# Writing a table of routing weights in 192 ordered parts instead of 24 large ones

## The chip, the cores and the metric

The kernel runs on one core of one Trainium2 chip. The metric is device time in microseconds (us). Before the change it is 3143.48 us, the median of three runs (3142.44 to 3146.86).

## The reference, cut to what matters

One transformer layer on 512 tokens of width 2048: a modulated norm, a mixer of attention and a linear recurrence, and then a layer of 16384 experts (PEER), of which each of 8 heads of a token chooses 16. The change lies in the expert layer:

```python
e = (jnp.take_along_axis(i1, ic // PEER_TOPK, axis=-1) * PEER_N_KEYS
     + jnp.take_along_axis(i2, ic % PEER_TOPK, axis=-1))
w = jax.nn.softmax(vs, axis=-1).astype(h.dtype)
...
ug = jnp.take(u, ex, axis=0)
act = jax.nn.gelu(jnp.einsum('thkd,td->thk', ug, hx)) * wx
vg = jnp.take(vt, ex, axis=0)
return jnp.einsum('thk,thkd->td', act, vg)
```

So an output row is a sum over the chosen experts of gelu(u . h) times the routing weight times a row of `v`.

## The kernel before, in words

The program is traced with a tile framework: pools hand out buffers, and every engine has its own in-order queue. The order within a queue is not the order of the source. The framework's scheduler (`schedule_with_timeline_sim`) lays it out by a model of time, moves an instruction ahead when its operands are ready in that model, and keeps true dependencies with semaphores. An instruction whose semaphore hasn't come holds up what stands behind it on its queue. Plain DMAs are issued from SyncE's queue (SP), indirect ones from GpSimd's (POOL).

The 512 tokens are four tiles of 128. Tile 0 of the expert layer takes its rows by direct gathers (`side_work`); three tiles go the dense way. For these the 16384 experts are 128 blocks of 128. `ublock(b)` computes gelu(u . h) of one block for 384 tokens: for each half of the 2048 columns, `stream` (line 96) loads 512 KB of `peer_u` into one of four `raw` buffers on SyncE (line 98), ScalarE casts it to `shi` (line 93), VectorE makes the rest `slo` (line 94), and TensorE runs 24 matmuls of 128x384 (line 689), three for each of 8 column groups: `shi` with `dh`, `shi` with `dl`, `slo` with `dh`. After each half `pump()` runs the lists in `todo`, which advance the direct gathers by GRATE = 0.9 (VectorE uses one gathered row with a pass of 128x2048, lines 755 and 757) and a list of scatters. After both halves ScalarE applies the gelu (line 693) and two DMAs on SyncE put the result into the DRAM tables `tab2` and `tab1` (lines 695 and 697). `ublocks(n)` runs blocks until n are done.

Beside each block's gelu values the tables hold the routing weights, half a tile of tokens (TH = 64) at a time. `halves_of` (line 892) builds them in `ws`, 128 x 128 x 64 floats, single-buffered, in 16 steps: one-hot matrices on VectorE (lines 906 and 911), four matmuls (line 912) and a copy (line 913) each, with ublocks between the steps. At the end four DMAs of 1 MB write `ws` to the table (line 917); each consists of 4096 runs of 256 bytes, and a maximum over the tokens is taken of each quarter (line 918). There are six such half tiles: four ahead of block 75, two after block 81. Between these, lines 928 to 938 do the top-k of the last tile, with loads of `s12` and four more blocks.

Nothing in this kernel pins the order on SyncE. When all blocks are done, the tables are gathered and multiplied with rows of `v` (line 988).

Of the kernel before, what the change touches and what calls it, by code (L numbers as in the profile page):

```python
# [58 lines left out]
def program(ctx: ExitStack, tc: tile.TileContext, a):  # L59
    nc = tc.nc  # L60
# [31 lines left out]
    def hilo(hi, lo, src):  # L92
        A.copy(hi, src)  # L93
        V.tensor_tensor(out=lo, in0=src, in1=hi, op=OP.subtract)  # L94

    def stream(src, n=1024):
        r = raw.tile([128, 1024], F32, name="raw")
        nc.sync.dma_start(r[:, :n], src)
        hi = hl.tile([128, 1024], F32R, name="shi")
        lo = hl.tile([128, 1024], F32R, name="slo")  # L100
        hilo(hi[:, :n], lo[:, :n], r[:, :n])
        return hi, lo

    def three(ah, al, bh, bl):
        return ((ah, bh), (ah, bl), (al, bh))

    def rstd(pool, ss, n, scale):
        v = pool.tile([128, 16], F32, name="rs", tag="rs", bufs=4)[:, :n]
        A.activation(v, ss, AF.Sqrt, bias=eps, scale=scale)
        V.reciprocal(v, v)  # L110
        return v
# [23 lines left out]
    for half in range(2):  # L135
        r = raw.tile([128, 1024], F32, name="raw")[:1]
# [28 lines left out]
    def bank():  # L165
        return ps.tile([128, 512], F32, name="ps", tag="ps")

    def pbank():
        return ps.tile([128, 512], F32, name="pj", tag="pj", bufs=2)

    for q in range(4):
        p = pbank()
# [7 lines left out]
    with tc.tile_pool(name="pro", bufs=1, reuse_waits="tile") as pro:  # L180
# [7 lines left out]
        for t in range(NT):  # L188
# [7 lines left out]
            r = rstd(pro, ss, 1, 1.0 / D)  # L196
            dg = pro.tile([128, 128], F32, name="dg", bufs=2)
            V.tensor_scalar(dg, ident, r, None, op0=OP.mult)
            for k4 in range(4):
                p = pbank()  # L200
# [7 lines left out]
        for k in range(KC):  # L208
            ada(1, k)
            ada(0, k)  # L210
            A.activation(xT[:, k], xT[:, k], AF.Identity, bias=mod[:, 0, k:k + 1], scale=gsc[0][:, k:k + 1])
            A.copy(hh[k], xT[:, k])
            V.tensor_tensor(out=hlo[k], in0=xT[:, k], in1=hh[k], op=OP.subtract)
            wh, wl = stream(a["w_pro"][k], PRO * 128)
            for i, (l, r) in enumerate(three(wfh, wfl, hh[k], hlo[k])):
                PE.matmul(pf[:8], l[:, k * 8:k * 8 + 8], r, start=(k == 0 and i == 0), stop=(k == KC - 1 and i == 2))
            for j in range(PRO):
                for i, (l, r) in enumerate(three(wh, wl, hh[k], hlo[k])):
                    PE.matmul(pacc[j], l[:, j * 128:j * 128 + 128], r, start=(k == 0 and i == 0),  # L219
                              stop=(k == KC - 1 and i == 2))  # L220
# [42 lines left out]
    p = pbank()  # L263
# [9 lines left out]
    p = bank()  # L273
# [19 lines left out]
    def proj(blk):  # L293
        p = pbank()
        b = W_AT[blk] - PRO
        for half in range(2):
            wh, wl = stream(a["w_in"][b, half])
            for k8 in range(8):
                k = half * 8 + k8
                for i, (l, r) in enumerate(three(wh, wl, hh[k], hlo[k])):  # L300
                    PE.matmul(p, l[:, k8 * 128:k8 * 128 + 128], r, start=(k == 0 and i == 0),  # L301
                              stop=(k == KC - 1 and i == 2))
        return p
# [215 lines left out]
    for q in range(4):  # L519
# [8 lines left out]
        for k2 in range(KC // 2):  # L528
            w = stream(a["w_out"][q, k2])
            if q == 3 and k2 >= KC // 2 - HELD:  # L530
                held += [(k2 * 2, *w), (k2 * 2 + 1, *w)]
                continue
            for k in (k2 * 2, k2 * 2 + 1):
                for t in range(NT):
                    out_mm(t, k, *w)
            if q < 3:
                some_ada(1)
        for t in range(NT):
# [10 lines left out]
            if q == 3:  # L549
                s4 = const.tile([128, 1], F32, name="s4", bufs=4)  # L550
                V.tensor_reduce(s4, ssq[:, t], axis=AX.X, op=OP.add)
                w = const.tile([128, 128], F32, name="dg", bufs=4)
# [6 lines left out]
    with tc.tile_pool(name="wk2", bufs=12, reuse_waits="tile") as wk2:  # L559
        for q in range(4):  # L560
            pr = bank()
            for k4 in range(4):
                k = q * 4 + k4
                p = bank()
# [80 lines left out]
    for h in range(H):  # L645
# [6 lines left out]
        for half in range(2):  # L652
            p = pbank()
# [10 lines left out]
            p = bank()  # L664
            c0 = half * 128
# [16 lines left out]
    def ublock(b):  # L682
        p = pbank()
        for half in range(2):
            uh, ul = stream(a["peer_u"][b, half])
            for k8 in range(8):
                k = half * 8 + k8
                for i, (l, r) in enumerate(three(uh, ul, dh[k], dl[k])):
                    PE.matmul(p[:, :NDT], l[:, k8 * 128:k8 * 128 + 128], r, start=(k == 0 and i == 0),  # L689
                              stop=(k == KC - 1 and i == 2))  # L690
            pump()
        ge = gq.tile([128, NDT], F32, name="ge")
        A.activation(ge, p[:, :NDT], AF.Gelu_apprx_tanh)  # L693
        rows = slice(128 + b * 128, 256 + b * 128)
        nc.sync.dma_start(tab2[rows].rearrange("p (t x) -> p t x", t=2)[:, :, 0:128],
                          ge[:, 128:384].rearrange("p (t x) -> p t x", t=2))
        nc.sync.dma_start(tab1[rows, 0:128], ge[:, 0:128])
# [6 lines left out]
    todo = []  # L704

    def pump():
        for f in todo:
            f()

    def ublocks(upto):  # L710
        while blk[0] < upto:
            ublock(blk[0])
            blk[0] += 1
# [76 lines left out]
    def scatter_some(n):  # L790
        for _ in range(n):
            if scatters:
                scatters.pop(0)()

    todo.append(lambda: side.send(GRATE))
    todo.append(lambda: scatter_some(1))
    for t in (1, 2):
# [34 lines left out]
    def make_list(lt, Fs, n):  # L832
# [5 lines left out]
        fs = [lt.tile([128, 128], F32, name=f"lu{i}") for i in range(len(Fs))]  # L838
        for f, F in zip(fs, Fs):
            V.scalar_tensor_tensor(out=f, in0=F, scalar=0.0, in1=iota1, op0=OP.is_gt, op1=OP.mult)  # L840
        if len(Fs) == 1:
# [51 lines left out]
    TH = 64  # L893
    sets = {}

    def halves_of(dz, t, o, tab, c0, lo, step):
        Fs = []
        for hf in range(2):
            h0 = hf * TH
            ws = dz.tile([128, NB, TH], F32, name="ws")  # L900
            for t4 in range(TH // 4):
                ublocks(lo + hf * step + t4 * (step - 3) // (TH // 4))
                p = bank()
                o1 = dz.tile([128, 4, 128], F32, name="o1", bufs=2)
                t0 = h0 + t4 * 4
                V.tensor_tensor(out=o1, in0=iota[:, None, :].to_broadcast([128, 4, 128]),
                                in1=o[:, 0, t0:t0 + 4, None].to_broadcast([128, 4, 128]), op=OP.is_equal)
                for j in range(4):
                    tt = t0 + j
                    o2 = dz.tile([128, 128], F32, name="o2", bufs=6)  # L910
                    V.tensor_scalar(o2, iota, o[:, 1, tt:tt + 1], o[:, 2, tt:tt + 1], op0=OP.is_equal, op1=OP.mult)
                    PE.matmul(p[:, j * 128:j * 128 + 128], o2, o1[:, j], start=True, stop=True)  # L912
                A.copy(ws[:, :, t4 * 4:t4 * 4 + 4].rearrange("p i t -> p t i"), p.rearrange("p (t i) -> p t i", t=4))
            F = dz.tile([128, NB], F32, name="F", bufs=4)
            for i in range(4):
                sl = slice(i * 32, i * 32 + 32)
                nc.sync.dma_start(tab[128 + i * 4096:4224 + i * 4096, c0 + h0:c0 + h0 + TH].rearrange("(i p) t -> p i t", p=128), ws[:, sl])
                V.tensor_reduce(F[:, sl], ws[:, sl], axis=AX.X, op=OP.max)
            Fs.append(F)
        V.tensor_tensor(out=Fs[0], in0=Fs[0], in1=Fs[1], op=OP.max)  # L920
        return Fs[0]

    with tc.tile_pool(name="dz", bufs=1, reuse_waits="tile") as dz:
        Fs = [halves_of(dz, t, oT[t], tab2, t * 256 + 128, B0 + 2 * t * BH, BH) for t in range(2)]
        sets[0] = make_list(dz, Fs, 0)
# [11 lines left out]
    with tc.tile_pool(name="dz2", bufs=1, reuse_waits="tile") as dz:  # L937
        sets[1] = make_list(dz, [halves_of(dz, 0, oT[2], tab1, 128, B0 + 4 * BH + 6, BL)], 1)
        ublocks(NB)
# [106 lines left out]
    def inv(t):  # L1046
        ss = fin.tile([128, 1], F32, name="fss", bufs=4)
        V.tensor_reduce(ss, ssf[:, t], axis=AX.X, op=OP.add)
        return rstd(fin, ss, 1, 1.0 / D)
# [63 lines left out]
    r = inv(1)  # L1113
# [75 lines left out]
```

## Time and profile before

| what | value |
| --- | --- |
| median of three runs | 3143.48 us |
| the profiled execution's own time | 3144.75 us |
| span of the profiled execution | 3142.9 us |
| TensorE's mean granted clock in it | 0.958 |
| starts of the 2048 matmuls with `slo` of the blocks, first and last | 1076.0 and 2382.1 us |
| the `peer_u` loads (SyncE) | 256, 512 KB each |
| writes of `ws` (SyncE) | 24, 1024 KB each |

Times in the profile count from the start of the span. PE is TensorE, PEld its weight load, DVE VectorE, ACT ScalarE, POOL GpSimd, SP SyncE; a "q" behind an engine's name is its instruction queue, where issuing a DMA or waiting on a semaphore takes place. In a row of a timeline stand the start, the duration, engine, line, operation, what it writes and reads, the count of instructions that were merged (xN), and in brackets the idle time before it and what ended it. A line such as L93 or L94 is that of a helper, so its rows are told apart by the tiles.

### The profile page before, as it was taken

The numbers are of one execution on the slowest core, as the hardware profiler recorded it, in microseconds if no ns is written. First come the engines' busy times: TensorE is split into PE (matmuls) and PEld (weight loads), VectorE is DVE, ScalarE is ACT, GpSimd is POOL, SyncE is SP. The second block draws the span as 40 slices with busy tenths as digits, with TensorE's granted clock in tenths as the row PEclk, the third lists the DMA queues.
The fourth block names the chain that finished last, engine by engine and source line by source line (L and its number), as shares of the span: only waits on it lengthen the run. The fifth ranks groups of instructions, "written<-read, shape, count | busy, mean of one in ns | idle before, by whom it ended". The sixth has DMA issues, their size and how long they took to land.

```text
span 3142.9 us, 39160 instructions
## 1 busy us (share of the span) xinstructions
PE 2872.5 (91%) x14093; PEld 2501.5 (80%) x14093; DVE 2487.0 (79%) x4100; ACT 1220.9 (39%) x1653; POOL 944.1 (30%) x673
## 2 busy tenths in 40 slices
PE   7899999989999999988878999889998899988887
PEld 5677777778788899988868999879996688766665
DVE  6877777763368899999989998968888866677787
ACT  5322223662232333433322343413223455556665
POOL 0000000000020033222242322264447645567774
PEclk9999899999999999999988999989999999999998
DMA  9867777333322389999989999989999977779896
GB/s 343 291 222 235 239 236 238 106 107 128 114 90 94 117 297 379 340 306 295 294 270 357 351 347 352 314 319 404 404 403 386 386 278 272 260 270 344 320 327 228
DMA packets 329503, 869.31 MB, mean 277 GB/s; under 512 B 125682, under 2 KB 181362, under 8 KB 274388
## 3 DMA queue, kind: packets, MB, share of 16 engines
q0 software_dynamic: 72512, 477.03, 40.4%
q1 hardware_dynamic: 256352, 389.52, 36.8%
q8 instruction: 112, 1.84, 0.2%
q14 instruction: 91, 0.75, 0.1%
q10 hardware_dynamic: 436, 0.18, 0.0%
HBM read 805.38 MB, written 61.25 MB: 276 GB/s over the span
## 4 chain that ended last, share of the span: by engine, by line
PE 53%; DVE 17%; DMA 15%; issue 8%; ACT 3%; POOL 2%; SPq 1%; DVEq 0%; POOLq 0%; ACTq 0%
PE pj L689 25%; DMA araw<-w_ada 8%; PE ps L988 7%; PE pj L659 6%; DVE slo L94 5%; PE ps L525 4%; DVE gr L757 3%; PE pj L301 2%; PE ps L219 2%; DMA raw<-tab,ig 2%; DVE araw L147 2%; PE ps L912 2%; PE pj L988 1%; PE pj L525 1%; DMA tab<-ws 1%
## 5 line engine op out<-in xcount | busy, mean ns | idle before, releaser
L689 PE MATMUL pj<-dh,slo 128*128 128x384 f32 x2048 | 698.3, 343 | 59.4 <-DVE slo L94 57.9
L689 PE MATMUL pj<-dh,shi 128*128 128x384 f32 x2048 | 699.1, 341 | 29.0 <-ACT shi L93 26.4
L689 PE MATMUL pj<-dl,shi 128*128 128x384 f32 x2048 | 694.8, 339 | 1.3 <-issue 1.3
L93 ACT CAST shi<-raw 128x1024 fp32r<-128x1024 f32 (+1 forms) x402 | 418.3, 1048 | 634.1 <-PE pj L689 219.0
L94 DVE TENSOR_TENSOR slo<-raw,shi 128x1024 fp32r<-128x1024 f32 (+1 forms) x402 | 485.1, 1214 | 214.3 <-ACT shi L93 200.1
L689 PEld LDWEIGHTS pj<-dh,slo 128*128 128x128 f32 x2048 | 392.1, 192 | 70.6 <-DVE slo L94 68.7
L94 DVE TENSOR_TENSOR slo<-gr,shi 128x1024 fp32r<-128x1024 f32 x342 | 407.2, 1220 | 39.6 <-ACT shi L93 38.1
L689 PEld LDWEIGHTS pj<-dh,shi 128*128 128x128 f32 x2048 | 393.0, 192 | 30.9 <-ACT shi L93 27.9
L93 ACT CAST shi<-gr 128x1024 fp32r<-128x1024 f32 x342 | 345.0, 1046 | 157.0 <-PE ps L988 99.2
L743 POOL DMA_INDIRECT gr<-u_rows,ei x128 | 196.0, 1531 | 690.5 <-DVE gr L757 319.6
L689 PEld LDWEIGHTS pj<-dl,shi 128*128 128x128 f32 x2048 | 392.3, 192 | 2.1 <-issue 2.0
L988 PE MATMUL ps<-shi,gh 128*128 128x512 f32 x740 | 277.7, 418 | 64.3 <-ACT gh L93 36.7
L147 DVE SCALAR_TENSOR_TENSOR araw<-araw,sil 128x1024 f32<-128x1024 f32 x192 | 233.7, 1222 | 104.8 <-DMA araw<-w_ada 101.5
L755 DVE SCALAR_TENSOR_TENSOR y<-gr,dots,y 128x2048 f32<-128x2048 f32 x128 | 300.3, 2346 | 13.9 <-DMA gr<-v_rows,ei 12.6
L988 PE MATMUL ps<-slo,gh 128*128 128x512 f32 x740 | 298.0, 411 | 14.6 <-DVE slo L94 13.8
L743 POOL DMA_INDIRECT gr<-v_rows,ei x128 | 211.7, 1654 | 311.4 <-DVE y L755 204.6
L757 DVE SCALAR_TENSOR_TENSOR gr<-gr,hrow 128x2048 f32<-128x2048 f32 x128 | 291.5, 2279 | 11.3 <-DMA gr<-u_rows,ei 8.8
L988 PE MATMUL ps<-shi,gl 128*128 128x512 f32 x740 | 273.8, 401 | 2.1 <-DVE gl L94 2.1
L678 POOL CAST dh<-hh 128x384 fp32r<-128x384 f32 x16 | 10.3, 645 | 857.8 <-DVE hh L572 857.8
L693 ACT ACTIVATE ge<-pj 128x384 f32<-128x384 f32 x128 | 63.0, 492 | 459.0 <-PE pj L689 371.1
L988 PEld LDWEIGHTS ps<-shi,gh 128*128 128x128 f32 x740 | 145.5, 198 | 112.2 <-ACT gh L93 45.7
L301 PE MATMUL pj<-hh,shi 128*128 128x512 f32 x528 | 215.6, 408 | 3.9 <-ACT w L477 3.5
(353 smaller groups left out, 4966.7 us busy)
## 6 DMA issues: line engine op xcount, KB each, us to landing
raw<-peer_u SPq DMA_DIRECT2D x256, 512.0 KB
araw<-w_ada SPq DMA_DIRECT2D x192, 512.0 KB
raw<-w_in SPq DMA_DIRECT2D x66, 512.0 KB
tab<-ws SPq DMA_DIRECT2D x24, 1024.0 KB
raw<-w_out SPq DMA_DIRECT2D x32, 512.0 KB
raw<-w_q SPq DMA_DIRECT2D x32, 512.0 KB
tab<-ge SPq DMA_DIRECT2D x128, 128.0 KB
tab<-ge SPq DMA_DIRECT2D x128, 64.0 KB
```

Source lines behind the costliest of these rows:

```text
L93: A.copy(hi, src)
L94: V.tensor_tensor(out=lo, in0=src, in1=hi, op=OP.subtract)
L147: V.scalar_tensor_tensor(out=r, in0=r, scalar=1.0, in1=sil[:, half * 1024:half * 1024 + 1024], op0=OP.mult, op1=OP.mult, accum_out=acc[:, ...
L301: PE.matmul(p, l[:, k8 * 128:k8 * 128 + 128], r, start=(k == 0 and i == 0), stop=(k == KC - 1 and i == 2))
L525: PE.matmul(po[t], l[:, ts], r[:, sl], start=(k == 0 and i == 0), stop=(k == KC - 1 and i == 2))
L659: PE.matmul(p, l[:, k8 * 128:k8 * 128 + 128], r, start=(k == 0 and i == 0), stop=(k == KC - 1 and i == 2))
L689: PE.matmul(p[:, :NDT], l[:, k8 * 128:k8 * 128 + 128], r, start=(k == 0 and i == 0), stop=(k == KC - 1 and i == 2))
L693: A.activation(ge, p[:, :NDT], AF.Gelu_apprx_tanh)
L743: G.indirect_dma_start(out=out, out_offset=None, in_=src, in_offset=bass.IndirectOffsetOnAxis(ap=idx, axis=0))
L755: V.scalar_tensor_tensor(out=y0, in0=r, scalar=dots[:, j:j + 1], in1=y0, op0=OP.mult, op1=OP.add)
L757: V.scalar_tensor_tensor(out=r, in0=r, scalar=1.0, in1=hrow, op0=OP.mult, op1=OP.mult, accum_out=dots[:, j:j + 1])
L988: PE.matmul(banks[t][half * 2 + q2], l[:, ts], x[:, sl], start=first and i == 0, stop=end and i == 2)
```

## The change

The four writes of a half tile become 32, each of 4 x 128 rows of the table (512 runs of 256 bytes, 128 KB). They are put on a list, `slices`, and `pump()` takes four from it first of all, behind each half of a block. Each write, and each load of `peer_u`, is pinned with `keep_in_program_order`: the framework adds an edge, without a semaphore, from the instruction that was traced last on the same engine's queue, so that the pinned one stands behind that one in issue order. The 16 steps of a half tile are spread over 13 blocks' worth of positions instead of 15, and the half tile's remaining blocks are run before the next half begins.

```diff
-    def stream(src, n=1024):
+    def stream(src, n=1024, pin=False):
         r = raw.tile([128, 1024], F32, name="raw")
-        nc.sync.dma_start(r[:, :n], src)
+        load = nc.sync.dma_start(r[:, :n], src)
+        if pin:
+            tc.keep_in_program_order(load)
...
-            uh, ul = stream(a["peer_u"][b, half])
+            uh, ul = stream(a["peer_u"][b, half], pin=True)
...
+    slices = []
+
+    def slices_some(n):
+        for _ in range(n):
+            if slices:
+                slices.pop(0)()
+
+    todo.append(lambda: slices_some(4))
...
-                ublocks(lo + hf * step + t4 * (step - 3) // (TH // 4))
+                ublocks(lo + hf * step + t4 * (step - 5) // (TH // 4))
...
+            def write(i, ws=ws, c=c0 + h0):
+                tc.keep_in_program_order(nc.sync.dma_start(
+                    tab[128 + i * 512:640 + i * 512, c:c + TH].rearrange("(i p) t -> p i t", p=128), ws[:, i * 4:i * 4 + 4]))
+
+            slices.extend([lambda i=i, w=write: w(i) for i in range(32)])
             for i in range(4):
                 sl = slice(i * 32, i * 32 + 32)
-                nc.sync.dma_start(tab[128 + i * 4096:4224 + i * 4096, c0 + h0:c0 + h0 + TH].rearrange("(i p) t -> p i t", p=128), ws[:, sl])
                 V.tensor_reduce(F[:, sl], ws[:, sl], axis=AX.X, op=OP.max)
+            ublocks(lo + hf * step + step)
```

## Rows read from the trace of the kernel before

**Rows 1.** The page: busy time of each engine over the span.
```profile
PE 2872.5 (91%) x14093; PEld 2501.5 (80%) x14093; DVE 2487.0 (79%) x4100; ACT 1220.9 (39%) x1653; POOL 944.1 (30%) x673
```

**Rows 2.** Matmuls with `slo`, line 689: ns (min/median/max), first and last start.
```profile
L689 PE MATMUL pj<-dh,slo x2048: 331/334/689, 1076.0 to 2382.1; 128*128 128x384 f32 x187
```

**Rows 3.** Stretches: all blocks, then the last 32; length, busy (instructions), clock, DMA.
```profile
core 0: us, PE busy (x) PEld busy (x) DVE busy (x) ACT busy (x) POOL busy (x), PEclk, DMA share, GB/s
1075.00:2383.00 1308.00, 1204.47 (x6961) 1186.59 (x6959) 1184.58 (x1645) 422.59 (x503) 444.25 (x283) 0.96 0.94 336
...
2108.00:2378.00 270.00, 268.21 (x1548) 267.44 (x1548) 225.50 (x131) 77.23 (x97) 123.01 (x69) 1.00 1.02 401
```

**Rows 4.** Timeline of SyncE's queue around the first half tile's writes.
```profile
1334.67 0.43 SPq L98 DMA_DIRECT2D raw<-peer_u  x1
1338.30 17.48 SPq L917 DMA_DIRECT2D tab<-ws  x4
1355.88 9.68 SPq L98 DMA_DIRECT2D raw<-peer_u  x1
```

**Rows 5.** Stretches around the six sets of writes: the first, and all six summed.
```profile
1338.00:1385.00 47.00, 36.65 (x213) 35.78 (x212) 43.55 (x75) 16.38 (x20) 8.48 (x6) 0.85 0.96 295
...
sum 282.00, PE 215.57 PEld 207.71 DVE 264.97 ACT 84.47 POOL 66.27; mean PE 35.93 PEld 34.62 DVE 44.16 ACT 14.08 POOL 11.05
```

**Rows 6.** Timeline of SyncE, ScalarE and VectorE in the steady stretch.
```profile
2296.77 0.48 ACT L693 ACTIVATE ge<-pj 128x384 f32<-128x384 f32 x1
...
2297.27 0.53 SPq L695 DMA_DIRECT2D tab<-ge  x1
...
2298.55 0.38 SPq L98 DMA_DIRECT2D raw<-peer_u  x1
...
2307.02 3.94 SPq L98 DMA_DIRECT2D raw<-peer_u  x3
2308.29 1.05 ACT L93 CAST shi<-raw 128x1024 fp32r<-128x1024 f32 x1 [1.61 <-PE pj L689]
2309.38 1.23 DVE L94 TENSOR_TENSOR slo<-raw,shi 128x1024 fp32r<-128x1024 f32 x1 [1.25 <-ACT shi L93]
2310.52 2.35 DVE L755 SCALAR_TENSOR_TENSOR y<-gr,dots,y 128x2048 f32<-128x2048 f32 x1
```

**Rows 7.** Timeline of SyncE at the end: last load, last blocks' stores.
```profile
2354.74 0.53 SPq L695 DMA_DIRECT2D tab<-ge  x1
...
2356.94 0.33 SPq L98 DMA_DIRECT2D raw<-peer_u  x1
2363.11 0.53 SPq L695 DMA_DIRECT2D tab<-ge  x1
...
2383.38 0.53 SPq L695 DMA_DIRECT2D tab<-ge  x1
```

**Rows 8.** Waits of SyncE's queue, 1075 to 2383 us: in total, times, longest (us).
```profile
SPq L695 <- ACT ge L693: 347.8, 99, 8.4
```

**Rows 9.** The chain that ended last: 512 KB loads of `w_ada`, start and us.
```profile
485.49 3.82 DMA araw<-w_ada
...
499.61 4.91 DMA araw<-w_ada
```

**Rows 10.** A `peer_u` load beside gathers, and the cast that waited for it.
```profile
1218.06 7.63 SPq L98 DMA_DIRECT2D raw<-peer_u  x3
...
1228.46 1.05 ACT L93 CAST shi<-raw 128x1024 fp32r<-128x1024 f32 x1 [1.80 <-DMA raw<-peer_u]
```

**Rows 11.** TensorE's idle stretch after the first writes and its restart: length, busy, clock.
```profile
1347.70:1352.60 4.90, 0.00 (x0) 0.74 1.00 228
1352.60:1356.60 4.00, 3.98 (x12) 0.50 1.32 309
```

**Rows 12.** SyncE's queue ahead of the blocks.
```profile
1041.39 5.80 SPq L98 DMA_DIRECT2D raw<-peer_u  x2
...
1074.03 0.38 SPq L721 DMA_DIRECT2D hrow<-hspill  x1
```

## The prediction

> **What bounds the kernel now.** The page comes first: TensorE is the busiest engine, but 91% is an average over stages [rows 1]. The change touches the blocks alone, whose matmuls start between 1076.0 and 2382.1 us [rows 2], a stage of 1306 us or 10.2 us a block. The view of stretches splits it. In the last 32 blocks TensorE is busy for 268.2 of 270 us at full clock: 1548 instructions, 0.173 us each, so a block of 48 matmuls is 8.3 us [rows 3]. Over all blocks it stands idle for 1308 - 1204.5 = 103.5 us, and VectorE, at 1184.6 us, is nearly as full [rows 3]. Part of the idle time belongs to the writes: the four of a half tile keep SyncE's queue for 17.48 us, and the load behind them for 9.68 us more [rows 4], so 27.2 us pass between two loads where a half block needs 4.2. In stretches of 282 us around the six sets TensorE is idle for 66.4 us, VectorE for only 17.0 [rows 5].
>
> The reader has to look at something else too: how far ahead the loads run. The last half block's load goes out at 2356.94, ahead of the stores of blocks 125 to 127 (two a block; the first at 2363.11, the last pair's at 2383.38) [rows 7]. So a load stands some two and a half blocks ahead in the queue, and TensorE never feels its latency. The stores are what SyncE waits for: it stood 347.8 us, 99 times, at a store for the gelu of its block [rows 8].
>
> **The change, part by part.** *The 32 small writes.* 27.2 us for 4 x 4096 runs and a load is 0.85 us for 512 runs, so four take 3.4 us of the queue per pump and one set eight pumps, four blocks. That is the same work, spread. The 17 and 27 us holes go. Half of the small writes stand between the two loads of a block and make the second 3.4 us later; 24 matmuls (4.2 us) cover that, so I cost it at nothing; without that cover it would be 24 blocks x 3.4 = 82 us. The next half tile's copies into `ws` wait until the writes have landed; two blocks stay for that: nothing. The other pins and the step - 5 move only issue order.
>
> *The pinned loads.* This is the part that decides. The load of a block's first half is pinned behind what was traced last on SyncE. In source order that is line 697 of the block before, a store which needs that block's gelu, which needs all its matmuls. SyncE is in order, so the load can't leave before TensorE is done with the previous block. Queued behind the waiting store are both loads (and the small writes); for them wait the cast, `slo`, and then TensorE. Blocks 0, 3 and 75 to 78 escape: what was traced last there is a load of `hrow`, the padding lists or `s12`. The other 122 become a chain:
>
> - matmuls 8.3 [rows 3];
> - gelu 0.5, begun an estimated 0.3 after the last matmul starts to drain (one is 0.33 long [rows 2], spaced 0.17);
> - two stores and the way to the load, 2297.27 to 2298.55: 1.3 [rows 6];
> - load to landing. Alone, no row shows it for `peer_u`. Lower bound: 3.8, the quickest of the `w_ada` loads shown, same size, while others were in flight. Upper: 10.4, from 1218.06 to the cast at 1228.46, beside gathers [rows 9, 10]. I take 5.0, near the second `w_ada` row (4.91): a block of about 20 us moves 1 MB of loads and some 1.8 MB of gathers, about 150 GB/s, far from the 336 to 401 GB/s of these stretches [rows 3];
> - cast 1.05, then `slo` 1.2 [rows 6], of which two matmuls (0.35) are hidden;
> - VectorE may just be in a pass of 2.35 [rows 6]: 0 to 2.35, I take 0.5, since it would stand idle half of the time;
> - the clock. After 4.90 us without a matmul TensorE ran 12 matmuls in 4.0 us at a granted clock of 0.50, the 1.2 GHz level, where 12 take 2.1 at 2.4 GHz [rows 11]: 1.9.
>
> Stall: 0.3 + 0.5 + 1.3 + 5.0 + 1.05 + 1.2 - 0.35 + 0.5 = 9.5. Block: 8.3 + 1.9 + 9.5 = 19.7 us. Stage: 122 x 19.7 + 6 x 10.2 = 2465 against 1306, so +1159. VectorE's 1184.6 us fit into it twice, and the gathers too. One thing more: block 0's load went out at 1041.39 and now stands behind the `hrow` load of 1074.03 [rows 12]; with 5.0 + 1.05 + 1.2 the blocks begin near 1082, +6. The holes at the writes lie inside the stage that is replaced, and are not counted again.
>
> Sum: +1165 on the profiled execution's 3144.75 us is 4310; that execution stands 1.3 above the median, so **4309 us**.
>
> On the latency the Trainium skill (DMA: Bandwidth & Descriptors, Anatomy of one DMA) says 2.0 us plus bytes/436 GB/s, fitted for GpSimd's path, an estimate of 3.2 us for 512 KB. By that the sum would be 122 x 1.8 = 220 lower, 4089; the rows of this kernel, 3.8 and up, are all longer.
>
> **The rivals.** *The loads still run ahead.* If the pins tie loads and writes only to each other, or the scheduler finds a way round the stores (say, by putting line 697 far later), the change does what its form suggests: 27 us holes become 3.4 us pieces. For it: the holes are there [rows 4, 5]. Against it: the edge is to the store by the words of the function, and SyncE's wait at that store is the longest in its view [rows 8]. The point that decides is whether a load can be issued before the gelu of the block before. Gain: between VectorE's idle time, 17, and TensorE's, 66; the middle, 42, gives 3102 us.
>
> *They run ahead and nothing comes of it.* VectorE is busy for 265 of 282 us in those stretches [rows 5]; if its 17 us aren't usable either, because the small writes' 3.4 us per half block meet the loads, the time stays at 3143.
>
> *The chain holds and the clock stays low.* If TensorE, idle for a third to half of the time, remains at 0.50, a block's matmuls are 48 x 0.33 = 15.9 us, a block 25.4: 122 x 25.4 + 61 - 1306 + 6 = +1860, 5003 us. For it: the restart was at 0.50 [rows 11]. Against it: with all the stalls that the stage has, its mean granted clock is 0.96 [rows 3], so the low level doesn't last.
>
> **How the numbers follow.** Forecast, the chain with a clock that recovers: 0.80. Chain with a low clock: 0.07. Loads run ahead and gain: 0.10. No change: 0.03. A measurement here tells about 0.2%, 6 us, from none; slower by more than that is 0.87, faster 0.10, within 0.03. With a landing of 3.8, no wait for VectorE and no clock loss a block is 8.3 + 7.8 = 16.1: 122 x 16.1 + 61 - 1306 + 6 = +725, 3868 us. With a landing of 8, between 5.0 and 10.4, and 1.5 for VectorE it is 23.7: +1652, 4795 us. Both upper ends at once (10.4 and 2.35) would be 26.95 a block, +2049, 5192; this corner, the low clock and the faster cases are the 2 in 10 left out.
>
> **What would show it.** In SyncE's queue: store, store, load, (four writes,) load, block after block, and never a load ahead of the gelu of the block before. In the waits: casts waiting for `peer_u` loads some 120 times, SyncE for the gelu some 120 times, up to about 17 us each. TensorE's stage about 2470 us long with about 1200 us idle, granted clock at 0.50 for some 4 us after each stall. The 1 MB writes of 3.6 to 13 us replaced by 192 of about 0.4 to 0.9. Wrong: three or four loads in a row before a store; then the first rival holds and all of the above is void. If the stalls are there but not near 9.5 us, the landing is the term to look at first, then `slo`.

## The result, and the profile after

The kernel after takes 4466.29 us (median of six runs, 4454.78 to 4479.26). Beside it the kernel before took 3142.96 us (six runs), a ratio of 1.4222 with a 95% interval of 1.4186 to 1.4258. The forecast was 4309 us, slower, with a range of 3868 to 4795: the direction and the mechanism came, and the time lies 157 us above the forecast. The profiled execution took 4463.39 us, with a span of 4461.5. Among the runs below, one of the ten executions of the kernel before with its stores moved took 7094.9 us, far from the other nine (3137 to 3155), and is left out of its ratio.

The page of the kernel after, busy time and granted clock over 40 slices (before: [rows 1]):

```profile
span 4461.5 us, 39414 instructions
...
PE 3173.7 (71%) x14093; PEld 2717.1 (61%) x14093; DVE 2510.0 (56%) x4100; ACT 1239.3 (28%) x1652; POOL 976.5 (22%) x673
...
PEclk9998999999577667777778777987877788999999
```

TensorE runs the same 14093 instructions, but they take 301 us more and the clock is low in the slices of the blocks alone (the row PEclk). The groups of instructions show where the time went; the row answers to [rows 2]:

```profile
L691 PE MATMUL pj<-dh,slo x2048: 331/334/689, 1079.3 to 3729.8; 128*128 128x384 f32 x187
```

The blocks' matmuls start over 2650 us instead of 1306, so +1344 lies in this stage, more than the +1319 between the two spans. The stretches of the kernel after (the columns are those of [rows 3]): the blocks up to block 3's stall, that stall, the blocks beside the direct gathers, the other blocks, and the stage behind them:

```profile
1077.00:1124.00 47.00, 24.12 (x99) 22.14 (x99) 42.30 (x96) 11.07 (x13) 7.38 (x5) 0.73 0.31 114
1124.00:1230.00 106.00, 15.25 (x67) 13.51 (x67) 95.57 (x99) 5.26 (x8) 59.02 (x31) 0.56 0.87 324
1230.00:2150.00 920.00, 475.07 (x2127) 436.26 (x2128) 701.11 (x657) 139.80 (x157) 402.84 (x222) 0.72 0.82 309
2150.00:3731.00 1581.00, 1004.15 (x4648) 935.04 (x4647) 408.73 (x808) 281.49 (x326) 48.06 (x49) 0.80 0.29 88
3731.00:4461.00 730.00, 651.87 (x2684) 511.53 (x2682) 515.72 (x729) 407.16 (x548) 438.41 (x330) 0.96 0.79 288
```

Over the first four stretches TensorE is busy for 1518.6 of 2654 us. No other engine has taken its place: VectorE, 1184.6 of 1308 us before [rows 3], is busy for 1247.7 of 2654, and for a quarter of the fourth stretch, in which the DMA engines too are idle for most of the time (0.29). Such a picture, with nothing full in the longest stretch, is that of a chain. The waits name its links. First SyncE's queue (total us, times, longest):

```profile
SPq L697 <- ACT ge L695: 1964.4, 123, 35.7
...
SPq L821 <- DVE padi L824: 69.4, 1, 69.4
```

Then the engines:

```profile
ACT shi L93 <- DMA raw<-peer_u: 903.3, 224, 15.5
PE pj L691 <- ACT shi L93: 894.4, 123, 17.1
```

SyncE waits 123 times at the first store (line 697, which was 695) for the gelu, 1964.4 us where it was 347.8 [rows 8]; the casts wait for `peer_u` and TensorE waits 123 times for a cast, 7.3 us a time. One turn of the chain in the fourth stretch (timeline of SyncE, ScalarE and VectorE, against [rows 6]):

```profile
2241.71 0.49 ACT L695 ACTIVATE ge<-pj 128x384 f32<-128x384 f32 x1 [9.51 <-PE pj L691]
2242.23 0.52 SPq L697 DMA_DIRECT2D tab<-ge  x1
2242.80 0.60 SPq L699 DMA_DIRECT2D tab<-ge  x1
2243.50 0.88 SPq L98 DMA_DIRECT2D raw<-peer_u  x2
2246.97 1.04 ACT L93 CAST shi<-raw 128x1024 fp32r<-128x1024 f32 x1 [4.77 <-DMA raw<-peer_u]
2248.05 2.51 DVE L94 TENSOR_TENSOR slo<-raw,shi 128x1024 fp32r<-128x1024 f32 x2 [14.59 <-ACT shi L93]
...
2258.76 0.49 ACT L695 ACTIVATE ge<-pj 128x384 f32<-128x384 f32 x1 [9.46 <-PE pj L691]
```

Read it from the top. Gelu, store, store, both loads of the next block, 3.5 us until the first cast starts, `slo`, and only then matmuls; 17.05 us later the next gelu. Before, the loads ran some two and a half blocks ahead [rows 7]; here not one half of the next block is loaded when the gelu starts.

### The profile page after: what moved, and what is told of

Same layout as the page of the kernel before. It is cut to its first block, busy times and chain, and to the rows that moved or that the text cites. A ratio compares the mean times of both kernels' runs of the same rounds, so it can differ in the third digit from the quotient of the medians.

```text
span 4461.5 us, 39414 instructions
## 1 busy us (share of the span) xinstructions
PE 3173.7 (71%) x14093; PEld 2717.1 (61%) x14093; DVE 2510.0 (56%) x4100; ACT 1239.3 (28%) x1652; POOL 976.5 (22%) x673
## 4 chain that ended last, share of the span: by engine, by line
PE 40%; DMA 22%; DVE 15%; issue 10%; ACT 5%; POOL 4%; SPq 3%; another core or an unknown queue 0%; ACTq 0%; DVEq 0%; POOLq 0%
PE pj L691 20%; DMA raw<-peer_u 10%; DVE slo L94 5%; PE ps L1003 4%; DMA araw<-w_ada 4%; PE pj L661 4%; POOL gr L745 4%; PE pj L303 3%; PE ps L527 3%; ACT shi L93 3%; DMA gr<-v_rows,ei 2%; DMA raw<-tab,ig 2%; DVE gr L759 2%; PE ps L221 2%; DMA raw<-tab,igown 1%
## 5 line engine op out<-in xcount | busy, mean ns | idle before, releaser
L691 PE MATMUL pj<-dh,shi 128*128 128x384 f32 x2048 | 810.7, 396 | 903.0 <-ACT shi L93 894.4
L691 PEld LDWEIGHTS pj<-dh,shi 128*128 128x128 f32 x2048 | 467.0, 228 | 940.2 <-ACT shi L93 929.4
L691 PE MATMUL pj<-dh,slo 128*128 128x384 f32 x2048 | 798.3, 390 | 64.0 <-DVE slo L94 63.7
L691 PE MATMUL pj<-dl,shi 128*128 128x384 f32 x2048 | 782.9, 382 | 0.0
L691 PEld LDWEIGHTS pj<-dh,slo 128*128 128x128 f32 x2048 | 454.9, 222 | 123.0 <-DVE slo L94 121.8
L691 PEld LDWEIGHTS pj<-dl,shi 128*128 128x128 f32 x2048 | 465.7, 227 | 0.0
L745 POOL DMA_INDIRECT gr<-u_rows,ei x128 | 226.2, 1767 | 479.8 <-PE pj L691 209.2
L745 POOL DMA_INDIRECT gr<-v_rows,ei x128 | 242.9, 1898 | 299.2 <-DVE y L757 191.6
L303 PE MATMUL pj<-hlo,shi 128*128 128x512 f32 x528 | 213.6, 405 | 0.0
L303 PE MATMUL pj<-hh,slo 128*128 128x512 f32 x528 | 212.2, 402 | 0.0
```

The lines of the kernel that those rows point to most:

```text
L745: G.indirect_dma_start(out=out, out_offset=None, in_=src, in_offset=bass.IndirectOffsetOnAxis(ap=idx, axis=0))
```

## The experiments

Each edit is against the kernel after, unless it says before. "Last matmul" is the last start of the blocks' `slo` matmuls; a block's time is worked out from the trace, from the last matmul of the block before it to its own last.

**The chain alone.** The pin of the first-half loads is put into the kernel before, and nothing else; the four 1 MB writes stay.

```diff
-            uh, ul = stream(a["peer_u"][b, half])
+            uh, ul = stream(a["peer_u"][b, half], pin=half == 0)
```

> The kernel before with its four large writes, and one thing added: the load of a block's first half is pinned. Theory: the chain alone makes the loss, 4400 to 4500 us, with the load behind the store in every block and casts waiting for peer_u loads some 115 times. Rival (the small writes make it): within 1% of 3143 us.

Measured: 4435.92 us (two runs), 1.4102 times before (1.405 to 1.4154). SyncE's waits in it:

```profile
SPq L697 <- ACT ge L695: 1956.1, 121, 35.4
...
SPq L813 <- DVE padi L816: 66.2, 1, 66.2
```

1293 of the 1323 us that the change costs are there with this one edge, and the two waits are nearly the same. The small writes, their pins, the pins of the second halves and the moved steps together add some 30 us to it.

**The chain taken away.** Only the second-half loads stay pinned; all else is the kernel after.

```diff
-            uh, ul = stream(a["peer_u"][b, half], pin=True)
+            uh, ul = stream(a["peer_u"][b, half], pin=half == 1)
```

> The changed kernel, but only the load of a block's second half is pinned (behind the first load or the small writes); the load of the first half is free again. Theory (the pin ties the first load to the store of the block before, and so to its gelu): loads run ahead, TensorE's stalls of 6 to 17 us per block go, the stage of the blocks comes back from 2653 us to about 1300, and the time to 3080 to 3150 us, 3102 by the prediction's gain of 42. Rival (the 192 small writes themselves, their descriptors and their landing, cost the time): over 4000 us still, since all 192 are there in the same order.

Measured: 3276.42 us, 1.0416 (1.0378 to 1.0453). The chain is gone: most blocks take 8.3 to 9.5 us again, and the wait at line 697 is 314.8 us in all. But the time lies 126 us above the bounds. Block 15 alone takes 150 us, block 95 takes 53, and some twenty others 12 to 25. SyncE's queue around block 15:

```profile
1230.09 1.41 SPq L826 DMA_DIRECT2D list<-padi  x2
1318.34 2.91 SPq L926 DMA_DIRECT2D tab<-ws  x4
1321.29 2.83 SPq L98 DMA_DIRECT2D raw<-peer_u  x1
1324.16 3.29 SPq L926 DMA_DIRECT2D tab<-ws  x4
```

A small write is pinned behind what was traced ahead of it, and a second-half load is pinned behind the write. The write has to wait for the last copy into `ws`; with the loads running ahead, SyncE reaches it long before that copy, and stands there with the load behind it (86.8 us between the first two rows, its longest wait for a copy into `ws`; 28.5 us at the padding DMAs came just before). In the kernel after no such wait stands among SyncE's long ones, presumably because its blocks are so slow that `ws` is ready first.

**The stores on another queue.** Both stores of a block's gelu go through ScalarE's queue. All pins stay, but what a load is pinned behind on SyncE's queue is then no store.

```diff
-        nc.sync.dma_start(tab2[rows].rearrange("p (t x) -> p t x", t=2)[:, :, 0:128],
+        nc.scalar.dma_start(tab2[rows].rearrange("p (t x) -> p t x", t=2)[:, :, 0:128],
...
-        nc.sync.dma_start(tab1[rows, 0:128], ge[:, 0:128])
+        nc.scalar.dma_start(tab1[rows, 0:128], ge[:, 0:128])
```

> The changed kernel with all pins, but the two stores of a block's gelu values are issued from ScalarE's queue instead of SyncE's. What was traced last on SyncE ahead of a first load is then a load or a small write. Theory: no chain, 3080 to 3150 us, and SyncE no longer waits for line 695. Rival (any pin of the loads costs, by the order as such): over 4000 us.

Measured: 3392.12 us, 1.0784 (1.0754 to 1.0815). This is what tells the store from the pin: with every load still in source order, 1074 of the 1323 us go as soon as the thing ahead of it doesn't wait for TensorE. The time is above the bounds again, and the waits between 1075 and 2700 us, two of SyncE's queue and one of ScalarE, say in part where:

```profile
SPq L821 <- DVE padi L824: 126.8, 1, 126.8
SPq L926 <- ACT ws L923: 64.5, 3, 26.7
...
ACT oT L734 <- PE ps L733: 136.6, 3, 48.7
```

Block 3 takes 141 us behind the padding DMA: the same kind of edge, with another instruction in front. Block 81 takes 69, and there it is no edge on SyncE: its two loads leave at 2105.2 and 2109.9 us, but its first cast starts at 2180.1, because ScalarE's queue stands for 40 us at a copy (line 734, the top-k of the last tile) that waits for TensorE, and TensorE for VectorE. Some twenty others take 12 to 28; they were not followed one by one.

**The same move in the kernel before.** The two stores go to ScalarE's queue there too.

> The kernel before, with the two stores of a block's gelu values issued from ScalarE's queue. No pins, four large writes. SyncE waited 348 us at these stores. Theory (where loads run two blocks ahead that wait costs nothing): within 1% of 3143 us, or slower, if ScalarE's casts queue behind the issue of the stores (1.1 us per block). Rival (SyncE's wait at the stores is what leaves the loads late around the large writes): 3080 to 3110 us.

Measured: 3141.75 us, 1.0017 (1.0 to 1.0035). So the 347.8 us that SyncE waits at the store in the kernel before [rows 8] cost nothing, because the loads run ahead of the stores there. The same wait is a cost or none by what stands behind it.

**Block 3's edge.** Only the first load of block 3 is not pinned.

```diff
-            uh, ul = stream(a["peer_u"][b, half], pin=True)
+            uh, ul = stream(a["peer_u"][b, half], pin=(b, half) != (3, 0))
```

> The changed kernel with one pin less: the first load of block 3, which stands behind the padding DMAs, is free. Theory: the 110 us between the last matmuls of blocks 2 and 3 are a wait of SyncE for the padding (69 us) that the prediction had passed over; block 3 comes down to some 25 us and the kernel to about 4380 us (85 less). Rival (VectorE was busy for 96 of 106 us there and the work has to be done before the half tiles anyway): the time moves to later blocks, 4450 to 4470 us.

Measured: 4417.44 us, 1.4026 (1.3977 to 1.4075), 49 us less than the kernel after and between theory and rival. In the profiled execution, at 4433.93 us the longest of the four, block 3 went from 109.8 us to 8.3, but blocks 4 to 38 from 25.7 to 26.7 on average and the later ones from 18.3 to 18.65, some 34 and 27 us in all. Part of the stall is therefore cover: gathers and VectorE's passes go on in it, and have to be done later where it is absent (the last gather is issued at 2178.9 us instead of 2147.3).

**The gathers beside the loads.** The first attempt set the rate of the direct gathers to nothing.

```diff
-GRATE = 0.9
+GRATE = 0.0
```

> The changed kernel with GRATE = 0: the 256 direct gathers of 1 MB, which the trace of the change shows beside blocks 4 to 38, are all left to the stage behind the blocks. Theory (those blocks take 25 us and not 18 because the load shares the DMA engines with gathers: 8 to 14 us from issue to cast against 3.4 to 4.4): blocks 4 to 38 come down to some 18 us, the last matmul of the blocks from 3730 to some 3500 us; the stage behind grows by more than that. Rival (other work beside these blocks, VectorE's, makes them slow): they stay at 25 us.

Measured: 4459.2 us in one run, and it tells nothing, for the gathers had not moved: the scheduler issued the last of them at 2147.9 us, in the kernel after at 2147.3. Asking for them later in the source doesn't make them later in the queue. The second attempt leaves the instructions and cuts the gathers' bytes to an eighth; VectorE's passes (their edits are left out here) read the short rows through `r8` at their old length.

```diff
+            r8 = r[:, None, :256].to_broadcast([128, 8, 256])
...
-                gather(r, a["v_rows" if v else "u_rows"], ei[:, j:j + 1])
+                gather(r[:, :256], a["v_rows" if v else "u_rows"].rearrange("r (a c) -> (r a) c", a=8), ei[:, j:j + 1])
```

> The changed kernel, with all pins; each direct gather brings 128 rows of 1 KB instead of 8 KB, and VectorE's passes stay 128x2048 long, over the 256 columns eight times (so tile 0's result is not the reference's). GRATE = 0 had not kept the gathers away from the blocks: the scheduler had put them in the same place. Theory (the loads of blocks 4 to 38 share the DMA engines with 1 MB gathers): their mean period falls from about 25 us to 18, the load to the cast from 8 to 14 us to about 4, the last matmul of the blocks from 3730 to about 3500, the kernel to about 4230 us. Rival (VectorE's passes beside these blocks): the period stays near 25 us, and the kernel over 4400 us.

Measured: 4198.54 us in one run. The stretches of this kernel over the same times as the second and third of the kernel after (it is further on by then: its block 38 ends before 1900 us):

```profile
1124.00:1230.00 106.00, 40.30 (x215) 36.40 (x214) 105.84 (x140) 22.16 (x25) 55.10 (x29) 0.70 0.23 74
1230.00:2150.00 920.00, 576.36 (x2634) 536.05 (x2633) 731.08 (x657) 158.32 (x180) 431.56 (x222) 0.78 0.36 107
```

VectorE has its 657 instructions as before, and the DMA engines' share falls from 0.82 to 0.36. From the start of a block's first load to its first cast it now takes 4.55 us on average over blocks 4 to 38, where it was 8.83, and a block 19.7 us where it was 25.7. Its second half comes sooner too: 11.9 us lie between a block's first matmul and its last, where they were 13.3. So 6.0 of the 7.4 us by which blocks 4 to 38 are longer than the later ones (18.3 us) come of the gathers' bytes. In the 1.4 that are left VectorE's work may have its part: `slo` starts 1.1 us after its cast has ended, on average, while VectorE is in other passes (1.85 us in the kernel after, 0.05 in its later blocks).

**The loads free, the writes pinned.** This is the change as its form suggests it, without the chain.

```diff
-            uh, ul = stream(a["peer_u"][b, half], pin=True)
+            uh, ul = stream(a["peer_u"][b, half])
```

> The changed kernel with all 32 small writes pinned as they are, and no load pinned. The run with the second loads pinned gave 3276 us, and its trace has one block of 150 us (15) and one of 53 us (95), in which the second load stood behind small writes whose half tile wasn't ready. Theory: that is its whole surplus; with the loads free the writes hold up at most what was put behind them by the scheduler, and the time is 3080 to 3150 us. Rival (the small writes cost something wherever they stand): 3200 us or more.

Measured: 3181.28 us, 1.0137 (1.0102 to 1.0172). It lies between the bounds of theory and rival, and above the kernel before: the parts bring nothing.

**No pins at all.** As the last one, and the writes are issued where the scheduler likes.

```diff
-                tc.keep_in_program_order(nc.sync.dma_start(
-                    tab[128 + i * 512:640 + i * 512, c:c + TH].rearrange("(i p) t -> p i t", p=128), ws[:, i * 4:i * 4 + 4]))
+                nc.sync.dma_start(
+                    tab[128 + i * 512:640 + i * 512, c:c + TH].rearrange("(i p) t -> p i t", p=128), ws[:, i * 4:i * 4 + 4])
```

> The changed kernel without any pin: 192 small writes where the scheduler puts them (in larger bunches: 32, 20, 24 in a row). Theory of the prediction's first rival (holes in the loads' queue are what the old writes cost, 42 us): bunched small writes make the same holes, so about 3143 us; if the spreading of the writes is worth something, this one is slower than the one with pinned writes. Rival (the size of a write matters, not its place): as fast as with pinned writes.

Measured: 3158.43 us, 1.0063 (1.0034 to 1.0093). Its interval lies below that of the kernel with pinned writes, so these pins cost some 0.7%, and what is left of the change still doesn't pay. The writes of the two kernels, first with the pins and then without:

```profile
L926 SPq DMA_DIRECT2D tab<-ws x192: 370/651/11132, 1338.2 to 2306.0; - x192
...
L926 SPq DMA_DIRECT2D tab<-ws x192: 359/574/6752, 1335.7 to 2089.5; - x192
```

Summed over the trace they hold SyncE's queue for 192 us with the pins and for 205 without; what differs is the place, the last one 217 us later.

**The old places of the steps.** The loads are free, the writes are pinned, and the 16 steps stand where they did before.

```diff
-                ublocks(lo + hf * step + t4 * (step - 5) // (TH // 4))
+                ublocks(lo + hf * step + t4 * (step - 3) // (TH // 4))
...
-            ublocks(lo + hf * step + step)
```

> The changed kernel with the 32 small writes pinned, the loads free, and the 16 steps of a half tile where the kernel before has them (step - 3, and no blocks run at the end of a half). The run with free loads and moved steps was 1.4% slower than before; its trace has the last half tile's writes at 2300 us, in the stretch that TensorE fills. Theory (the moved steps are its surplus, and the parts are worth little, as VectorE is the bound beside them): 3130 to 3150 us, the same as before within 0.3%. First rival of the prediction (the holes are worth 42 us): 3090 to 3110 us. Rival (the pinned parts cost): 3170 us or more.

Measured: 3182.2 us, 1.0151 (1.0126 to 1.0176), the same as with the steps moved: moving them is not what costs. The row of its writes and that of its last matmuls:

```profile
L926 SPq DMA_DIRECT2D tab<-ws x192: 365/636/8587, 1333.9 to 2323.5; - x192
...
L691 PE MATMUL pj<-dh,slo x2048: 331/334/689, 1071.8 to 2421.1; 128*128 128x384 f32 x187
```

And the writes of the kernel before (one row of its groups, in full form):

```profile
L917 SPq DMA_DIRECT2D tab<-ws x24: 377/3562/13072, 1338.3 to 2038.5; - x24
```

The blocks end 39 us later than at 2382.1 [rows 2], most of the 44 that are lost. Summed over the trace, the 192 writes hold SyncE's queue for 206 us, the 24 large ones for 110, and the last of them is issued at 2323.5 instead of 2038.5, in the stretch that TensorE filled before [rows 3]. The kernel without pins narrows it down: there the small writes hold the queue for as long (205 us) but end as early as 2089.5, and 17 us are lost instead of 44. So the larger part goes with the pins of the writes, of which the trace shows the later place. Whether the queue's time makes the rest stays open.

## Why the prediction was right, and where it was off

**The mechanism** was right. The load of a first half is pinned behind the store at the end of the block before, the store waits for the gelu, the gelu for TensorE. The edge alone gives 1293 of 1323 us, and moving the stores off the queue takes away 1074. The Trainium skill (DMA: Bandwidth & Descriptors, Anatomy of one DMA) says that a wait for a semaphore happens on the issuing sequencer, ahead of dispatch; the 1964.4 us at line 697, with loads behind it that hardly wait for anything themselves (line 98 adds up to some 32 us in this stage), agree. Counted were 122 blocks of 19.7 us; there were 121, of 20.6 on average. Block 81, counted as chained, took 8.3: its loads left right behind block 80's. Why is open.

**The mis-sized terms** can be read off the turn of the chain above. In the later blocks (39 to 127, 84 of them chained, 18.3 us on average against 19.7):

- Between the start of the last matmul and the gelu 0.38 (0.3 foreseen), from the gelu's start to the load 1.78 (0.5 + 1.3): right.
- From load to cast a median of 3.83 us (mean 3.95), where the landing was put at 5.0. **This is the term of the sum that failed**, and in both directions: too long here, by 1.1 us a block on average, and far too short earlier.
- First cast to first matmul 1.10, to the end of `slo` 2.30 (1.05 + 1.2): right. Hardly a wait for VectorE is seen in these turns (0.05 on average), where 0.5 was allowed.
- The clock, 1.9, and the part of `slo` that isn't hidden, 0.85, can only be measured together: from its first matmul to its last a block takes a median of 10.8 us (10.2 in the quickest turn) and 8.15 where it is unchained, 2.6 more against 2.75. Near.

The stretches around one such turn (idle time; the first 4 us of matmuls; the rest of the block):

```profile
2241.40:2248.00 6.60, 0.28 (x2) 0.00 (x0) 0.00 (x0) 1.52 (x2) 0.00 (x0) 0.78 0.55 189
2248.00:2252.00 4.00, 3.68 (x11) 3.18 (x12) 2.45 (x2) 1.06 (x2) 0.00 (x0) 0.52 0.00 0
2252.00:2258.50 6.50, 6.50 (x39) 6.40 (x37) 0.00 (x0) 0.00 (x0) 0.00 (x0) 1.00 0.00 0
```

After 6.6 us of idling, 11 matmuls begin in 4 us at a granted clock of 0.52, the 1.2 GHz level; the other 37 run at 1.00, the 2.4 GHz level (the row's 39 take in two that began before). It is as at the restart in the kernel before [rows 11], now in block after block. The third rival, a clock that stays low, fell with it.

**Beside the gathers** the landing was 8.83 us on average over blocks 4 to 38, and one block 25.7 us. The step of the prediction that failed is the sentence "a block of about 20 us moves 1 MB of loads and some 1.8 MB of gathers, about 150 GB/s". The gathers were not spread over the blocks as before, when they ran from 1127.0 to 2459.3 us, beside nearly all of them. They went on while the blocks stood (groups of line 745 in the kernel after):

```profile
L745 POOL DMA_INDIRECT gr<-u_rows,ei x128: 932/1906/3053, 1110.6 to 1605.7; - x128
L745 POOL DMA_INDIRECT gr<-v_rows,ei x128: 932/2080/3664, 1607.9 to 2147.3; - x128
```

All 256 fell beside blocks 2 to 38, with 309 GB/s in the third stretch and 88 GB/s behind it. Beside them a load that is waited for takes this long (timeline of the kernel after):

```profile
1417.92 0.49 ACT L695 ACTIVATE ge<-pj 128x384 f32<-128x384 f32 x1 [8.05 <-PE pj L691]
...
1419.71 1.04 SPq L98 DMA_DIRECT2D raw<-peer_u  x2
...
1427.75 1.04 ACT L93 CAST shi<-raw 128x1024 fp32r<-128x1024 f32 x1 [9.34 <-DMA raw<-peer_u]
```

The prediction's lower bound, 3.8, is the median without gathers; beside them the landing is 3.5 to 14.2 us, in six of 35 blocks above the upper bound of 10.4 [rows 10]. What failed was to take one value for both. The experiment with the small gathers shows the cause. Of the 6.0 us a block that were missing, 3.8 are the landing; most of the rest lies behind the first matmul, 13.3 us to the last where the later blocks take 11.0, with `slo` 1.85 us late behind VectorE's other passes (0.5 was allowed) and the second half's cast late as well. The Trainium skill's fit (DMA: Bandwidth & Descriptors, Anatomy of one DMA) gave an estimate of 3.2 us. The quickest load here took 3.34 with its twin 0.5 us behind it, so the fit is near where no gathers run; it has no term for other traffic. The sum by it, 4089, would have been further off than the one by the rows.

**Block 3** was named as one that escapes. It is the reverse: its load is pinned behind the DMAs of the padding list, and these wait for VectorE (SyncE's queue, kernel after):

```profile
1139.92 0.62 SPq L699 DMA_DIRECT2D tab<-ge  x1
1209.97 0.32 SPq L821 DMA_DIRECT2D tab<-pad  x1
...
1210.85 1.40 SPq L826 DMA_DIRECT2D list<-padi  x2
1212.30 1.05 SPq L98 DMA_DIRECT2D raw<-peer_u  x2
```

69 us of silence, and a block of 109.8 us where 10.2 was counted; 20 more lie between the load and its cast at 1232.48, ahead of which ScalarE copies into `ws`. With this one pin gone the block took 8.3 us. That the thing ahead is not a store was no reason to call it free; what it waits for had to be asked. Blocks 0 and 75 to 78 did escape.

**The small writes at nothing** held where the DMA engines are quiet and did not beside the gathers. SyncE's queue in the kernel after, first beside the gathers, then behind them:

```profile
1521.52 0.44 SPq L98 DMA_DIRECT2D raw<-peer_u  x1
1522.01 12.07 SPq L926 DMA_DIRECT2D tab<-ws  x4
1534.18 2.73 SPq L98 DMA_DIRECT2D raw<-peer_u  x1
...
3133.01 0.40 SPq L98 DMA_DIRECT2D raw<-peer_u  x1
3133.46 2.44 SPq L926 DMA_DIRECT2D tab<-ws  x4
3136.00 1.15 SPq L98 DMA_DIRECT2D raw<-peer_u  x1
```

Four writes take 2.44 us here (2.4 to 2.5 in all 32 sets behind the gathers), below the 3.4 foreseen, and 12.07 there (2.5 to 15.0 in the 16 sets beside them). The 3.4 had counted the 9.68 us of the load behind the large writes as theirs [rows 4]; 17.48 us for the same bytes give 2.2 for four. The eight blocks with writes beside gathers (15 to 18, 33 to 36) took 27.2 us on average, the other 27 took 25.3: some 15 us, if it is the writes, for single blocks scatter from 21.0 to 31.5. The cover by the first 24 matmuls held for the most part: from the first matmul to the last these eight took 13.6 us against 13.2. They lost ahead of it, 10.4 us from the first load to its cast against 8.4.

**The sum, put right.** From the foreseen end of the stage at 3547 us (1076 + 2465 + 6) to the last matmul at 3729.8 it is +183: block 3 +100, blocks 4 to 38 at 25.7 instead of 19.7 +211, the 84 later ones at 18.3 instead of 19.7 -115, blocks 1 and 2 +9, the unchained ones -19 (8.3 instead of 10.2 for 75 to 78; block 81 11 less), the start -3. Behind the blocks 30 us come back, since that stage is 730 us long and was 760 (2383 to the end of the span at 3143), most likely because the direct gathers, whose last was issued at 2459.3 before, are done by 2147.3: argued, not tried. That leaves +153 on the profiled execution (4463 against 4310), which is the miss. It is this small in part by luck: terms of +320 and of -167 stand against each other.

**The first rival**, loads that run ahead and a gain of 42 us, fell twice: the loads don't run ahead, and where they are made to, the time is 3181 or 3158 us, not 3102. The second rival, loads ahead and nothing gained (3143), comes nearest to those runs. TensorE's idle time around the large writes [rows 4, 5] was no store of time that smaller writes could open. No version that was tried beats the kernel before.

## What to carry to other kernels

Before an instruction is pinned on an in-order queue, write down what will stand ahead of it and what that waits for; a prefetch pinned behind a store of the step before is no prefetch. Look for it in SyncE's waits and in the order store, load, store, load of its timeline, with no engine full. And price a load that comes onto the critical path by what else is on the DMA engines at that time, as the trace shows it, not by one number for the stage.

## What the runs showed of the hardware

The same pair of 512 KB loads reached its first cast in 3.8 us (median) while the DMA engines moved 88 GB/s, in 8.83 us (mean, 3.5 to 14.2) while gathers of 1 MB ran beside them, 309 GB/s in all, and in 4.55 us (mean) when these gathers carried an eighth of the bytes. What had not been expected is how strongly issue on the queue follows: four writes of 512 runs of 256 bytes held SyncE's queue for 2.44 us in the quiet stretch and for 12.07 us beside gathers, so a DMA's cost on its queue is not a property of the DMA alone. With gathers of 1 MB beside them splitting made it dearer: 192 small writes held the queue for 206 us (in the kernel with the old places of the steps) where 24 large ones with the same bytes took 110. In the chained kernels, 192 held it for 190 us, and for 112 when the gathers were cut to an eighth.
